# RMSNorm factors as fp32r products of two halves, and earlier sums for the feed-forward norm, in a two-layer decoder

## The chip, the cores and the metric

The kernel runs on one core of a Trainium2 chip. The metric is the device time of one execution in microseconds (us). The median of three runs of the kernel before is 2770.46 us (2770.25 to 2772.49). One further execution was recorded by the profiler, and everything read from a trace below comes from that one.

The core's engines run side by side and each takes its own instructions in order: TensorE (PE) multiplies matrices, and its weight loads are shown apart as PEld; VectorE (DVE) and ScalarE (ACT) do elementwise work; GpSimd (POOL) does a few small operations here; SyncE's queue (SP) issues the transfers. An instruction that waits for another engine holds up everything behind it on its own engine.

## The reference

Two layers, 2048 features, 256 tokens. Each layer mixes tokens (an SSD mixer in layer 0, forgetting attention in layer 1), then has a SwiGLU feed-forward block of 5632 hidden features and a gate that adds a projected per-layer input. Six kinds of RMSNorm stand around them:

```python
def rmsnorm(x, w):
    return x * lax.rsqrt(jnp.mean(x * x, axis=-1, keepdims=True) + EPS) * w

for i in range(DEPTH):
    hn = rmsnorm(h, norm_mix_pre[i])
    mix = ssd_mixer(...) if i % 2 == 0 else fox_mixer(...)
    h = h + rmsnorm(mix, norm_mix_post[i])
    ff = swiglu(rmsnorm(h, norm_ffn_pre[i]), w_gate, w_up, w_down)
    h = h + rmsnorm(ff, norm_ffn_post[i])
    pe = rmsnorm(p[i] @ ple_w_proj[i], ple_norm[i])
    h = h + jax.nn.sigmoid(h @ ple_w_gate[i]) * pe
```

The SSD mixer also normalizes its 4096 inner features in 8 groups of 512, and multiplies by a weight behind that. All is float32.

## The kernel before

**Data.** Activations lie transposed: a chunk is a tile of 128 features by 256 tokens, 16 chunks (h0 to h15) make the residual. A matrix product is made to float32 precision from fp32r products of two halves: a weight tile raw is cast to fp32r on ACT (wh, L181), and the rest raw minus wh is formed on DVE (wl, L186); an activation x likewise has a high half and a low half side by side in 512 columns. The high weights then multiply both halves (128x512, L243) and the low weights the high half (128x256, L245). ACT and DVE take the two halves of the result out of PSUM: a copy (tb, L270) and an addition (L271).

**Units and stages.** A unit is a group of up to six output chunks that are accumulated in PSUM side by side. A stage is one weight tile of a unit, with its transfer, its cast wh, its wl and its products. Units follow each other without a break, so that the next unit's first stages run while the last unit's results are still taken out. Weight tiles have numbers in the order of their use (wl264, wh548).

**What is done beside the products.** Small tasks stand in a queue, `bg`, and a few are popped with each stage. `paced` puts a task's DVE operation behind the wl of a stage that is named by `low`, `lag` does the same for ACT's side, `turn` holds the next wl behind a task's last operation. So the order on DVE and ACT is laid down by hand: a task that is popped a stage earlier stands ahead of another wl.

**A norm.** Squares of the 16 chunks are made on ACT (L293) and added on DVE (L294) into one tile (ssb, ssp for the per-layer projection, gss for the mixer's groups). `rstd_small` sums that tile over its 128 partitions by products whose stationary operand is the tile's half and whose moving operand is one column of ones (L314, float32), scales the sums on DVE (ms, L317) and raises them to the power -0.5 on POOL (rs, L320). `rstd_wide` spreads the factors of 256 tokens over all partitions: DVE makes two diagonal matrices (dg, L326), and a float32 product with a tile of ones gives 128x256 (L330), which ACT copies out (rwide, rpe or grw, L333). The trace shows each call of either as four hardware products, since it splits a float32 product in two. There are 18 calls of each.

**The places that the change touches.**

- The update unit is the first unit of the feed-forward block. While its products run, DVE makes the new residual from the mixer's normalized output: per chunk a scaling (sg, L458), an addition (h, L462) and the low half of the next block's input (x, L473); ACT makes the high half (L467).
- Behind it `late_norm` computes the feed-forward norm beside the next unit, the up unit: four pops of four squares and sums, `f1` with the column sum (wl263 to wl265), and `f2` with the wide product and the copy; then half of the factor (rwide2, L517), and the gate's silu in pops (L551 to L558). The norm's factor is applied to the results, since it is a factor per token.
- The per-layer norm (`pe_small`, `pe_wide`) runs beside the gate's units at the end of each layer, where the next chunks of h are formed (pp, L652; h, L656) once its factor rpe is there.
- The mixer's eight group norms (`gate_tasks`), the norm behind the mixer and the one behind the feed-forward block (`post_norm`, with `rstd_small` and `rstd_wide`), and the first norm of each layer.

Of the kernel before, what the change touches and what calls it, by code (L numbers as in the profile page):

```python
# [56 lines left out]
def tile_trunk(ctx, tc, a, out):  # L57
# [24 lines left out]
    ident, tri3, nstril, bigm = cst[:, 0:128], cst[:, 128:512], cst[:, 512:640], cst[:, 640:768]  # L82
    ones = cp.tile([P, P], F32, name="ones")
# [227 lines left out]
    def rstd_small(acc, n):  # L311
        ps = misc()
        for j in range(2):
            PE.matmul(ps[:, j:j + 1], lhsT=acc[:, j * P:(j + 1) * P], rhs=ones[:, :1],  # L314
                      start=True, stop=True)
        ms = tmp("ms", (P, 2))
        dmark[0] = V.tensor_scalar(out=ms, in0=ps[:, :2], scalar1=1.0 / n, scalar2=EPS,  # L317
                                   op0=mult, op1=add)
# [4 lines left out]
    def rstd_wide(rs, o):  # L323
        dg = tmp("dg", bufs=1)
        for j in range(2):
            dmark[0] = V.tensor_scalar(out=dg[:, j * P:(j + 1) * P], in0=ident,  # L326
                                       scalar1=rs[:, j:j + 1], scalar2=None, op0=mult)
        ps = misc()
        for j in range(2):
            PE.matmul(ps[:, j * P:(j + 1) * P], lhsT=ones, rhs=dg[:, j * P:(j + 1) * P],  # L330
                      start=True, stop=True)
# [31 lines left out]
    A.activation(warm, mhalf, AF.Exp)  # L363

# [137 lines left out]
    def mk_r(half=True, small=None, pin=False):  # L502
        r = []

        def f1():
            r.append(rstd_small(ssb, D))
# [5 lines left out]
        def f2():  # L512
            rstd_wide(r[0], rwide)
            if pin:
                lag[1].append(mark[0])
            if half:
                V.tensor_scalar(out=rwide2, in0=rwide, scalar1=0.5, scalar2=None, op0=mult)  # L517
        return f1, f2
# [19 lines left out]
    def tail(i, mpx, m, pp, mk_next):  # L538
# [3 lines left out]
        with ExitStack() as st:  # L542
# [24 lines left out]
            def late_norm():  # L567
                f1, f2 = mk_r(pin=True)
                bg.extend(sums_of(ssb, h, range(NCH), (4, 4, 4, 4)))
                bg.extend((f1, noop, f2, noop))  # L570
# [65 lines left out]

        def pe_small():
            r_pe.append(rstd_small(ssp, D))
            turn.append(dmark[0])
# [108 lines left out]
    def prep0(c):  # L748
        if c + 3 < NCH:
            load_x(c + 3)  # L750
        if c == 8:
            nc.sync.dma_start(out=cst, in_=a["cst"])
        split(h[c], xs0[c], col("mix_pre0", c))
        sumsq(ssb, h[c], c == 0)

    with ExitStack() as ys:
        yp = pool(ys, "yp", side="right")
        y = [yp.tile([P, T], F32, name=f"y{c}") for c in range(32)]
        with ExitStack() as st:
# [166 lines left out]
            def gate_tasks(g, S):  # L926
# [392 lines left out]
```

## Time and profile before

| | |
|---|---|
| median of three runs | 2770.46 us |
| the profiled execution | 2772.22 us |
| its span on the core | 2770.4 us |
| PE busy | 2759.2 us (100% of the span) |
| DVE busy | 1914.8 us (69%) |
| ACT busy | 1483.5 us (54%) |
| POOL busy | 50.3 us (2%) |
| granted TensorE clock | 1.0 in every slice |

A row of the timeline gives the start, the duration and the count of equal instructions in a row, and in brackets how long the engine was idle before and which instruction ended that. The ends of products are modelled and overlap the next start by some tenths of a microsecond, so distances of starts tell more than durations: a 128x512 product and the next start 0.23 us apart, a 128x256 fp32r product and the next 0.117 us. The idle time in brackets is by the same reason somewhat shorter than the time that the queue of products loses. On DVE an operation's successor starts some 0.08 us before the duration of the first is over.

### The profile page before, as it was taken

To read this page: it belongs to the slowest core of one execution; us is meant where nothing else is said; L and a number is where in the kernel's file an instruction comes from. 1 tells how busy PE (TensorE), PEld (TensorE's weight loads), DVE (VectorE), ACT (ScalarE), POOL (GpSimd) and SP (SyncE) were. 2 spreads that over 40 slices of the span, in tenths; PEclk is the share of its full clock that TensorE was granted. 3 is DMA by queue.
4 is the path that set the end of the run, shared out by engine and by line. 5 is a ranking of instruction groups with operands and counts; after the bars stand their busy time and mean duration, and the time that the engine had idled before them with its cause. 6 is when DMAs were issued, how large, how long until landed. Compare 5 with 4: busy or idle time off the path is not lost.

```text
span 2770.4 us, 43140 instructions
## 1 busy us (share of the span) xinstructions
PE 2759.2 (100%) x16342; PEld 2451.2 (88%) x16342; DVE 1914.8 (69%) x3145; ACT 1483.5 (54%) x2455; POOL 50.3 (2%) x104
## 2 busy tenths in 40 slices
PE   9999999999999999999999999999999999999999
PEld 8888888889888888888898998889888888888898
DVE  8888878755876645666668756766876545666577
ACT  6586676554654444444546544555654444445454
POOL 0000000000000000000000000000000000000000
PEclk9999999999999999999999999999999999999999
DMA  7665655565566555656545676545656556656544
GB/s 252 191 197 185 190 189 176 158 211 181 158 214 192 190 190 187 190 181 194 193 163 200 184 211 193 179 156 165 201 187 194 190 191 185 193 171 200 202 162 165
DMA packets 262512, 520.10 MB, mean 188 GB/s; under 512 B 17392, under 2 KB 42128, under 8 KB 262304
## 3 DMA queue, kind: packets, MB, share of 16 engines
q1 hardware_dynamic: 258640, 504.96, 57.5%
q0 software_dynamic: 3520, 12.15, 1.4%
q8 instruction: 128, 2.10, 0.3%
q14 instruction: 80, 0.66, 0.1%
q10 hardware_dynamic: 144, 0.24, 0.0%
HBM read 515.10 MB, written 2.18 MB: 187 GB/s over the span
## 4 chain that ended last, share of the span: by engine, by line
PE 97%; DVE 2%; ACT 1%; issue 0%; DMA 0%; SPq 0%; DVEq 0%; ACTq 0%
PE acc L243 56%; PE acc L245 30%; PE acc L240 1%; PE acc L239 1%; PE acc L238 1%; PE acc L232 1%; PE acc L233 1%; PE acc L234 1%; DVE wl L186 1%; PE mi L914 1%; PE mi L916 0%; PE mi L330 0%; PE mi L881 0%; PE mi L1152 0%; PE mi L1188 0%
## 5 line engine op out<-in xcount | busy, mean ns | idle before, releaser
L243 PE MATMUL acc<-x,wh 128*128 128x512 f32 x5008 | 1708.4, 394 | 5.3 <-DVE g L271 2.3
L186 DVE TENSOR_TENSOR wl<-raw,wh 128x1024 fp32r<-128x1024 f32 (+4 forms) x1020 | 1173.0, 1155 | 743.7 <-ACT wh L181 742.9
L181 ACT CAST wh<-raw 128x1024 fp32r<-128x1024 f32 (+4 forms) x1020 | 1006.3, 993 | 968.4 <-PE acc L243 851.6
L245 PE MATMUL acc<-x,wl 128*128 128x256 f32 x5008 | 1329.4, 283 | 0.2
L243 PEld LDWEIGHTS acc<-x,wh 128*128 128x128 f32 x5008 | 926.3, 188 | 190.6 <-issue 3.8
L245 PEld LDWEIGHTS acc<-x,wl 128*128 128x128 f32 x5008 | 932.2, 189 | 26.4 <-issue 2.1
L243 PE MATMUL acc<-a,wh 128*128 128x512 f32 x1232 | 425.5, 391 | 0.0
L245 PE MATMUL acc<-a,wl 128*128 128x256 f32 x1232 | 342.3, 282 | 0.0
L243 PEld LDWEIGHTS acc<-a,wh 128*128 128x128 f32 x1232 | 230.0, 188 | 46.5
L245 PEld LDWEIGHTS acc<-a,wl 128*128 128x128 f32 x1232 | 233.2, 189 | 2.2
L243 PE MATMUL acc<-xb,wh 128*128 128x512 f32 x512 | 181.9, 397 | 0.0
L270 ACT COPY tb<-acc 128x256 f32<-128x256 f32 (+1 forms) x401 | 140.2, 369 | 45.2 <-PE acc L245 27.3
L245 PE MATMUL acc<-xb,wl 128*128 128x256 f32 x512 | 146.0, 285 | 0.0
L243 PEld LDWEIGHTS acc<-xb,wh 128*128 128x128 f32 x512 | 96.0, 188 | 19.1
L245 PEld LDWEIGHTS acc<-xb,wl 128*128 128x128 f32 x512 | 97.0, 189 | 0.7 <-issue 0.2
L243 PE MATMUL acc<-xq,wh 128*128 128x512 f32 x224 | 77.7, 391 | 0.0
L896 ACT ACTIVATE E<-ab,bias 128x128 f32<-128x128 f32 x192 | 59.7, 390 | 13.7 <-PE mi L916 12.7
L271 DVE TENSOR_TENSOR g<-acc,tb 128x256 f32<-128x256 f32 x172 | 66.1, 417 | 0.6
L825 DVE SCALAR_TENSOR_TENSOR g<-xr,vec,g 128x256 f32<-128x256 f32 x144 | 63.3, 479 | 1.5 <-ACT g L822 0.8
L245 PE MATMUL acc<-xq,wl 128*128 128x256 f32 x224 | 63.1, 282 | 0.0
L320 POOL TENSOR_TENSOR rs<-ms,mhalf 128x2 f32<-128x2 f32 x18 | 24.4, 1356 | 1926.8 <-DVE ms L317 1926.8
L294 DVE TENSOR_TENSOR ssb<-ssb,sq 128x256 f32<-128x256 f32 x120 | 50.6, 422 | 12.0 <-ACT sq L293 8.1
(219 smaller groups left out, 2198.1 us busy)
## 6 DMA issues: line engine op xcount, KB each, us to landing
raw<-down SPq DMA_DIRECT2D x176, 512.0 KB, 4.1
raw<-ssd_in SPq DMA_DIRECT2D x152, 512.0 KB, 4.5
raw<-gate SPq DMA_DIRECT2D x128, 512.0 KB, 4.4
raw<-up SPq DMA_DIRECT2D x128, 512.0 KB, 4.4
raw<-fox_in SPq DMA_DIRECT2D x64, 512.0 KB, 4.1
raw<-gate SPq DMA_DIRECT2D x64, 384.0 KB, 3.2
raw<-up SPq DMA_DIRECT2D x64, 384.0 KB, 3.5
raw<-ssd_out SPq DMA_DIRECT2D x40, 512.0 KB, 4.3
```

Of the source, the lines that this page charges most:

```text
L181: low_a[0] = A.copy(out=wh[:, :kc * n], in_=raw[:, :kc * n])
L186: low[0] = V.tensor_tensor(out=wl[:, :kc * n], in0=raw[:, :kc * n], in1=wh.bitcast(F32)[:, :kc * n], op=sub)
L232: PE.matmul(o, lhsT=xh, rhs=wh[:, c, :], start=st, stop=False)
L233: PE.matmul(o, lhsT=xh, rhs=wl[:, c, :], start=False, stop=False)
L234: PE.matmul(o, lhsT=x[:, 1, t * P:(t + 1) * P], rhs=wh[:, c, :], start=False, stop=sp)
L243: PE.matmul(accs[t], lhsT=wh[:, c, t * P:(t + 1) * P], rhs=x.rearrange("p a n -> p (a n)"), start=st, stop=False)
L245: PE.matmul(accs[t][:, :T], lhsT=wl[:, c, t * P:(t + 1) * P], rhs=x[:, 0, :], start=False, stop=sp)
L270: i = A.copy(out=tb[:np_], in_=acc[:np_, T:2 * T])
L271: took[0] = (i, V.tensor_tensor(out=o, in0=acc[:np_, :T], in1=tb[:np_], op=add))
L294: last_v[0] = V.tensor_tensor(out=acc, in0=acc, in1=sq, op=add)
L825: V.scalar_tensor_tensor(out=c, in0=xr[:, k:k + T], scalar=col(f"conv_w{k}", cc), in1=c, op0=mult, op1=add)
L896: A.activation(E[:, i, b * P:(b + 1) * P], ab[:, i, lo:lo + P], AF.Relu, scale=-1.0, bias=bias3[:, b, h0 + i:h0 + i + 1])
```

## The change

The change has three parts.

- The wide product (`rstd_wide`): the factors are split on DVE into fp32r halves (rh and rl, 128x2 each). Instead of two diagonal matrices against ones, each half's column is taken as a stationary operand by broadcasting, against an fp32r identity (identr): four fp32r products. All 18 calls are changed.
- The column sum (`rstd_small`): 12 of the 18 calls get the tile split first, by a cast on ACT (`hi`) and a subtraction on DVE (`lo`), and each half's columns are summed by an fp32r product with two columns of ones: again four products. These are the 8 groups of the mixer, the 2 feed-forward norms and the 2 per-layer norms. The other 6 stay as they were.
- The order: of the feed-forward norm's 16 squares, 9 are popped during the update unit (after 13 empty pops) instead of behind it; behind it stand 4 and 3, then `f0` (hi), `f1` (lo and the column sum), `f2a` (the wide product alone), an empty pop and `f3` (the copy and rwide2, placed by hand). In the per-layer norm two more sums move ahead into the unit before, hi is its own pop, and the rest follows.

The diff, cut (line numbers of the kernel after are higher by 2 at L186, by 20 or so behind `rstd_wide`):

```diff
+    def halves(acc):
+        s = [tmp("sq", dt=F32R, bufs=4), tmp("sq", dt=F32R, bufs=4)]
+        def hi(pin=False):
+            with after(low_a[0]) if pin else nullcontext():
+                mark[0] = A.copy(out=s[0], in_=acc)
+            if pin:
+                lag[1].append(mark[0])
+        def lo():
+            last_v[0] = V.tensor_tensor(out=s[1], in0=acc, in1=s[0].bitcast(F32), op=sub)
+        return s, hi, lo
...
+    def rstd_small(acc, n, s=None):
...
+                for i in range(2):
+                    PE.matmul(ps[:, 2 * j:2 * j + 2], lhsT=s[i][:, js], rhs=onesr, start=i == 0,
+                              stop=i == 1)
...
     def rstd_wide(rs, o):
-        dg = tmp("dg", bufs=1)
-        for j in range(2):
-            dmark[0] = V.tensor_scalar(out=dg[:, j * P:(j + 1) * P], in0=ident,
-                                       scalar1=rs[:, j:j + 1], scalar2=None, op0=mult)
+        rr = [tmp("rh", (P, 2), F32R), tmp("rl", (P, 2), F32R)]
+        V.tensor_copy(out=rr[0], in_=rs)
+        dmark[0] = V.tensor_tensor(out=rr[1], in0=rs, in1=rr[0].bitcast(F32), op=sub)
         ps = misc()
         for j in range(2):
-            PE.matmul(ps[:, j * P:(j + 1) * P], lhsT=ones, rhs=dg[:, j * P:(j + 1) * P],
-                      start=True, stop=True)
+            for i in range(2):
+                PE.matmul(ps[:, j * P:(j + 1) * P],
+                          lhsT=rr[i][:, j:j + 1].broadcast_to((P, P)), rhs=identr,
+                          start=i == 0, stop=i == 1)
...
             def late_norm():
-                f1, f2 = mk_r(pin=True)
-                bg.extend(sums_of(ssb, h, range(NCH), (4, 4, 4, 4)))
-                bg.extend((f1, noop, f2, noop))
+                chain = mk_r(pin=True)
+                bg.extend(sums_of(ssb, h, range(9, NCH), (4, 3)))
+                bg.extend(chain)
...
+                    if first[0]:
+                        assert not bg
+                        bg.extend([noop] * 13 + sums_of(ssb, h, range(9), (3, 3, 3)))
...
-        pops0 = [noop] * 14 + [ssp_of(8, 9), ssp_of(10, 11)]
-        pops1 = [seq(ssp_of(12, 13), t1(0, 1)), seq(ssp_of(14, 15), t1(2, 3)),
+        pops0 = [noop] * 13 + [ssp_of(8, 9), ssp_of(10, 11), ssp_of(12, 13)]
+        pops1 = [seq(ssp_of(14, 15), t1(0, 1)), seq(pe_hi, t1(2, 3)),
                  seq(pe_small, t1(4, 5), t2(0, 1)), t2(2, 3), seq(pe_wide, t2(4, 5))]
```

How the instructions stand is shown at three places; each also occurs in layer 1. A row is the line, the operation, what it writes and what it reads; the numbers behind a tile's name tell instances apart.

**DVE, the feed-forward norm in layer 0** (mi is the column sum's result in PSUM). Before:

```order
L186 TENSOR_TENSOR wl264_8328<-raw264_8325,wh264_8327 128x768
L317 TENSOR_SCALAR ms_812_8346<-mi_811_8343 128x2
L186 TENSOR_TENSOR wl265_8353<-raw265_8350,wh265_8352 128x768
L186 TENSOR_TENSOR wl266_8371<-raw266_8368,wh266_8370 128x768
L186 TENSOR_TENSOR wl267_8397<-raw267_8394,wh267_8396 128x768
L326 TENSOR_SCALAR dg_814_8386<-cst_80,rs_813_8348 128x128 x2
L517 TENSOR_SCALAR rwide2_139<-rwide_138 128x256
L186 TENSOR_TENSOR wl268_8415<-raw268_8412,wh268_8414 128x768
L551 TENSOR_TENSOR sg_778_8177<-sg_778_8177,rwide2_139 128x256
```

After:

```order
L188 TENSOR_TENSOR wl263_8395<-raw263_8392,wh263_8394 128x768
L323 TENSOR_TENSOR sq_825_8309<-ssb_143,sq_824_8308 128x256
L337 TENSOR_SCALAR ms_840_8416<-mi_839_8411 128x2
L188 TENSOR_TENSOR wl264_8423<-raw264_8420,wh264_8422 128x768
L188 TENSOR_TENSOR wl265_8450<-raw265_8447,wh265_8449 128x768
L188 TENSOR_TENSOR wl266_8468<-raw266_8465,wh266_8467 128x768
L345 CAST rh_842_8438<-rs_841_8418 128x2
L346 TENSOR_TENSOR rl_843_8439<-rs_841_8418,rh_842_8438 128x2
L552 TENSOR_SCALAR rwide2_142<-rwide_141 128x256
L188 TENSOR_TENSOR wl267_8488<-raw267_8485,wh267_8487 128x768
```

The scaling ms stood behind wl264, and stands ahead of it now; rwide2, which reads the copied factor, stood behind wl267 and stands ahead of it now. On PE the column sum's last products stand as before right ahead of the first use of wl264, and the wide product stands ahead of the last of wl266's six low products, where it stood behind the first of wl267's.

**DVE, the end of the update unit in layer 0**, whose x_745 (before: x_720) is the last low half. Before:

```order
L473 SCALAR_TENSOR_TENSOR x_719_7686<-h14_97,vec_79,x_719_7686 128x256
L458 SCALAR_TENSOR_TENSOR sg_777_8106<-m0_15_6601,vec_79,rwide_138 128x256
L462 TENSOR_TENSOR h15_98<-h15_98,sg_777_8106 128x256
L186 TENSOR_TENSOR wl257_8125<-raw257_8122,wh257_8124 128x768
L473 SCALAR_TENSOR_TENSOR x_720_7687<-h15_98,vec_79,x_720_7687 128x256
L186 TENSOR_TENSOR wl258_8144<-raw258_8141,wh258_8143 128x768
L186 TENSOR_TENSOR wl259_8150<-raw259_8147,wh259_8149 128x768
L271 TENSOR_TENSOR sg_778_8177<-acc_756_7794,tb_779_8178 128x256
L271 TENSOR_TENSOR sg_780_8181<-acc_757_7795,tb_781_8182 128x256
```

After:

```order
L495 SCALAR_TENSOR_TENSOR x_744_7765<-h14_99,vec_79,x_744_7765 128x256
L480 SCALAR_TENSOR_TENSOR sg_803_8188<-m0_15_6680,vec_79,rwide_141 128x256
L484 TENSOR_TENSOR h15_100<-h15_100,sg_803_8188 128x256
L188 TENSOR_TENSOR wl257_8207<-raw257_8204,wh257_8206 128x768
L296 TENSOR_TENSOR ssb_143<-ssb_143,sq_804_8224 128x256
L495 SCALAR_TENSOR_TENSOR x_745_7766<-h15_100,vec_79,x_745_7766 128x256
L296 TENSOR_TENSOR ssb_143<-ssb_143,sq_805_8227 128x256
L188 TENSOR_TENSOR wl258_8233<-raw258_8230,wh258_8232 128x768
L188 TENSOR_TENSOR wl259_8239<-raw259_8236,wh259_8238 128x768
L296 TENSOR_TENSOR ssb_143<-ssb_143,sq_806_8266 128x256
L273 TENSOR_TENSOR sg_812_8284<-acc_782_7876,tb_813_8285 128x256
L273 TENSOR_TENSOR sg_814_8288<-acc_783_7877,tb_815_8289 128x256
```

Three sums into ssb now stand among the last low half, wl258, wl259 and the first addition that frees a PSUM tile, and more among the additions behind.

**DVE and PE, the per-layer norm in layer 0**, DVE first (gz are results of the gate, taken out of PSUM). Before:

```order
L648 SCALAR_TENSOR_TENSOR pp0_4_6606<-gz_1295_15493,pp0_4_6606 128x256
L648 SCALAR_TENSOR_TENSOR pp0_5_6607<-gz_1297_15497,pp0_5_6607 128x256
L326 TENSOR_SCALAR dg_1310_15644<-cst_80,rs_1309_15592 128x128 x2
L186 TENSOR_TENSOR wl547_15656<-raw547_15653,wh547_15655 128x1024
L652 SCALAR_TENSOR_TENSOR pp0_0_6602<-pp0_0_6602,vec_79,rpe_142 128x256
L656 TENSOR_TENSOR h0_83<-h0_83,pp0_0_6602 128x256
L186 TENSOR_TENSOR wl548_15681<-raw548_15678,wh548_15680 128x1024
```

After:

```order
L188 TENSOR_TENSOR wl547_15759<-raw547_15756,wh547_15758 128x1024
L345 CAST rh_1342_15744<-rs_1341_15692 128x2
L346 TENSOR_TENSOR rl_1343_15745<-rs_1341_15692,rh_1342_15744 128x2
L273 TENSOR_TENSOR gz_1345_15833<-acc_1331_15601,tb_1346_15834 128x256
L273 TENSOR_TENSOR gz_1347_15837<-acc_1332_15602,tb_1348_15838 128x256
L699 SCALAR_TENSOR_TENSOR pp0_0_6681<-pp0_0_6681,vec_79,rpe_145 128x256
L703 TENSOR_TENSOR h0_85<-h0_85,pp0_0_6681 128x256
L188 TENSOR_TENSOR wl548_15784<-raw548_15781,wh548_15783 128x1024
```

PE, where the wide product stands. Before:

```order
L245 MATMUL acc_1299_15501<-x_1229_14976,wl546_15625 128x256
L243 MATMUL acc_1300_15502<-x_1228_14975,wh546_15624 128x512
L330 MATMUL mi_1311_15647<-dg_1310_15644,ones_81 128x128 x2
L245 MATMUL acc_1300_15502<-x_1228_14975,wl546_15625 128x256
L243 MATMUL acc_1300_15502<-x_1229_14976,wh546_15624 128x512
L245 MATMUL acc_1300_15502<-x_1229_14976,wl546_15625 128x256
```

After:

```order
L247 MATMUL acc_1333_15603<-x_1259_15068,wl547_15759 128x256
L350 MATMUL mi_1344_15748<-identr_81,rl_1343_15745 128x128
L350 MATMUL mi_1344_15748<-identr_81,rh_1342_15744 128x128
L350 MATMUL mi_1344_15748<-identr_81,rl_1343_15745 128x128
L245 MATMUL acc_1333_15603<-x_1260_15069,wh547_15758 128x512
L247 MATMUL acc_1333_15603<-x_1260_15069,wl547_15759 128x256
L247 MATMUL acc_1334_15604<-x_1259_15068,wl547_15759 128x256
L245 MATMUL acc_1334_15604<-x_1260_15069,wh547_15758 128x512
L247 MATMUL acc_1334_15604<-x_1260_15069,wl547_15759 128x256
L245 MATMUL acc_1355_15851<-x_1245_15054,wh548_15783 128x512
L245 MATMUL acc_1356_15852<-x_1245_15054,wh548_15783 128x512
L247 MATMUL acc_1353_15849<-x_1245_15054,wl548_15784 128x256
```

Between the wide product and the first use of wl548 stood 29 products, and 7 stand there now. On DVE wl548 stands behind the first product with rpe (pp) and the addition into h0, as before; in layer 1 it is behind two of each and one more addition out of PSUM.

## Rows read from the trace of the kernel before

**Rows 1.** The page: its span, busy time by engine, chain that ended last.

```profile
span 2770.4 us, 43140 instructions
...
PE 2759.2 (100%) x16342; PEld 2451.2 (88%) x16342; DVE 1914.8 (69%) x3145; ACT 1483.5 (54%) x2455; POOL 50.3 (2%) x104
...
PE 97%; DVE 2%; ACT 1%; issue 0%; DMA 0%; SPq 0%; DVEq 0%; ACTq 0%
```

**Rows 2.** Waits of PE: us in total, times, longest.

```profile
PE acc L243 <- DVE g L271: 2.3, 2, 1.2
PE acc L243 <- ACT wh L181: 1.8, 3, 0.6
```

**Rows 3.** Groups by line and shape: busy us, mean ns, idle before.

```profile
L243 PEld LDWEIGHTS acc<-x,wh 128*128 128x128 f32 x5008 | 926.3, 188 | 190.6 <-issue 3.8 <-DVE g L271 2.7 <-ACT wh L181 2.5
...
L330 PEld LDWEIGHTS mi<-dg,ones 128*128 128x128 f32 x72 | 10.3, 190 | 0.6
```

**Rows 4.** Timeline (start, duration, count) of PE: wide product, per-layer norm, layer 0.

```profile
1498.98 0.61 PE L330 MATMUL mi<-dg,ones 128*128 128x128 f32 x4
...
1499.54 0.40 PE L243 MATMUL acc<-x,wh 128*128 128x512 f32 x1
```

**Rows 5.** Timeline of PE, a float32 product of 256 columns (L1152).

```profile
1680.63 0.60 PE L1152 MATMUL mi<-k,q 128*128 128x256 f32 x2
...
1681.18 0.39 PE L243 MATMUL acc<-xb,wh 128*128 128x512 f32 x1
```

**Rows 6.** Timeline of DVE and PE, behind the feed-forward norm's column sum in layer 0.

```profile
750.46 0.16 DVE L317 TENSOR_SCALAR ms<-mi 128x2 f32<-128x2 f32 x1
750.50 0.73 PE L245 MATMUL acc<-x,wl 128*128 128x256 f32 x4
750.54 0.96 DVE L186 TENSOR_TENSOR wl<-raw,wh 128x768 fp32r<-128x768 f32 x1
```

**Rows 7.** Timeline of PE, ACT and DVE, that norm's wide product and copy.

```profile
757.01 0.61 PE L330 MATMUL mi<-dg,ones 128*128 128x128 f32 x4
...
757.65 0.37 ACT L333 COPY rwide<-mi 128x256 f32<-128x256 f32 x1 [6.93 <-PE mi L330]
...
758.06 0.29 DVE L517 TENSOR_SCALAR rwide<-rwide 128x256 f32<-128x256 f32 x1 [4.43 <-ACT rwide L333]
758.81 0.95 PE L243 MATMUL acc<-x,wh 128*128 128x512 f32 x3 [0.60 <-ACT wh L181]
```

**Rows 8.** Timeline of PE, the end of the up unit.

```profile
770.82 0.86 PE L245 MATMUL acc<-x,wl 128*128 128x256 f32 x6
772.84 0.50 PE L243 MATMUL acc<-x,wh 128*128 128x512 f32 x1 [1.16 <-DVE g L271]
```

**Rows 9.** By stretch: length, busy PE, PEld, DVE, ACT, POOL, clock, DMA share, GB/s.

```profile
758.06:772.36 14.30, 13.02 (x74) 11.07 (x72) 13.76 (x26) 9.96 (x17) 0.00 (x0) 1.00 0.69 223
716.00:735.00 19.00, 19.00 (x108) 16.29 (x107) 18.65 (x35) 11.79 (x21) 0.00 (x0) 1.00 0.67 181
```

**Rows 10.** Timeline of DVE, the end of the update unit in layer 0.

```profile
732.97 0.48 DVE L473 SCALAR_TENSOR_TENSOR x<-h,vec,x 128x256 fp32r<-128x256 f32 x1
...
735.24 0.75 DVE L271 TENSOR_TENSOR sg<-acc,tb 128x256 f32<-128x256 f32 x2
```

**Rows 11.** Timeline of DVE, first results of the gate's first unit, layer 0.

```profile
1479.90 0.42 DVE L294 TENSOR_TENSOR ssp<-ssp,sq 128x256 f32<-128x256 f32 x1
1480.24 0.75 DVE L271 TENSOR_TENSOR gz<-acc,tb 128x256 f32<-128x256 f32 x2
```

**Rows 12.** Timeline of DVE behind the per-layer norm's copy, layer 0.

```profile
1500.03 0.48 DVE L652 SCALAR_TENSOR_TENSOR pp<-pp,vec,rpe 128x256 f32<-128x256 f32 x1 [3.22 <-ACT rpe L333]
...
1500.89 1.22 DVE L186 TENSOR_TENSOR wl<-raw,wh 128x1024 fp32r<-128x1024 f32 x1
```

**Rows 13.** Timeline of PE and DVE, the per-layer norm's wide product, layer 1.

```profile
2727.15 0.61 PE L330 MATMUL mi<-dg,ones 128*128 128x128 f32 x4
...
2728.99 0.76 DVE L656 TENSOR_TENSOR h<-h,pp 128x256 f32<-128x256 f32 x2
```

More of the change, by code (lines that the diff above doesn't have):

```diff
@@ L309, in paced @@
         return r
-    def rstd_small(acc, n):
+    def halves(acc):
[9 more added lines that the diff above has]
+    def rstd_small(acc, n, s=None):
         ps = misc()
         for j in range(2):
-            PE.matmul(ps[:, j:j + 1], lhsT=acc[:, j * P:(j + 1) * P], rhs=ones[:, :1],
-                      start=True, stop=True)
+            js = slice(j * P, (j + 1) * P)
+            if s is None:
+                PE.matmul(ps[:, j:j + 1], lhsT=acc[:, js], rhs=ones[:, :1], start=True, stop=True)
+            else:
+                for i in range(2):
+                    PE.matmul(ps[:, 2 * j:2 * j + 2], lhsT=s[i][:, js], rhs=onesr, start=i == 0,
+                              stop=i == 1)
         ms = tmp("ms", (P, 2))
-        dmark[0] = V.tensor_scalar(out=ms, in0=ps[:, :2], scalar1=1.0 / n, scalar2=EPS,
-                                   op0=mult, op1=add)
+        dmark[0] = V.tensor_scalar(out=ms, in0=ps[:, :2] if s is None else ps[:, :4:2],
+                                   scalar1=1.0 / n, scalar2=EPS, op0=mult, op1=add)
         rs = tmp("rs", (P, 2), bufs=3)
@@ L363, in tile_trunk @@
     A.activation(warm, mhalf, AF.Exp)
+    A.copy(out=onesr, in_=ones[:, :2])
     def load_x(c):
@@ L503, in mk_r, with f0 @@
         r = []
+        s, hi, lo = halves(ssb) if pin else (None, None, None)
+        def f0():
+            hi(True)
         def f1():
-            r.append(rstd_small(ssb, D))
+            if pin:
+                paced(lo)
+            r.append(rstd_small(ssb, D, s))
             if pin:
@@ L513, in f2, with f2a, f3, halved @@
             rstd_wide(r[0], rwide)
-            if pin:
-                lag[1].append(mark[0])
             if half:
                 V.tensor_scalar(out=rwide2, in0=rwide, scalar1=0.5, scalar2=None, op0=mult)
-        return f1, f2
+        def f2a():
+            r.append(rstd_wide(r[0], None))
+        def f3():
+            with after(low_a[0]):
+                lag[1].append(A.copy(out=rwide, in_=r[1]))
+            def halved():
+                last_v[0] = V.tensor_scalar(out=rwide2, in0=rwide, scalar1=0.5, scalar2=None,
+                                            op0=mult)
+            paced(halved)
+        return (f0, f1, f2a, noop, f3) if pin else (f1, f2)
     def out_units(sizes, rhs, m_of, pre=None):
@@ L635, in ssp_of, with pe_hi @@
             return f
+        hs = []
+        def pe_hi():
+            hs.extend(halves(ssp))
+            hs[1](True)
         def pe_small():
-            r_pe.append(rstd_small(ssp, D))
+            paced(hs[2])
+            r_pe.append(rstd_small(ssp, D, hs[0]))
             turn.append(dmark[0])
@@ L752, in prep0 @@
             nc.sync.dma_start(out=cst, in_=a["cst"])
+        if c == 12:
+            A.copy(out=identr, in_=ident)
         split(h[c], xs0[c], col("mix_pre0", c))
@@ L926, in gate_tasks, with gn0 @@
             def gate_tasks(g, S):
+                def gn0():
+                    S["s"], hi, S["lo"] = halves(S["ss"])
+                    hi()
                 def gn1():
-                    S["rs"] = rstd_small(S["ss"], 512)
+                    S["lo"]()
+                    S["rs"] = rstd_small(S["ss"], 512, S["s"])
                 def gn2():
```

7 lines of the change are left out of this document (4 added, 3 removed).

## Prediction

> **What bounds the kernel now.** I read the page first. PE is busy for the whole span and the chain that ended last is 97% PE [rows 1], so the time is what PE's queue takes, plus its gaps. An edit elsewhere counts only where it makes PE wait or spares it a wait. The waits of PE come next: the two largest are the addition that frees a PSUM tile (2.3 us in 2 places) and the cast wh (1.8 us in 3) [rows 2]. Both belong to the feed-forward norm, so I looked there on the timeline of each engine. Lastly I asked where DVE has no room. In the up unit's silu pops it works 13.76 of 14.30 us, in the update unit 18.65 of 19.00 [rows 9], and the change puts or moves DVE work into both.
>
> **The products themselves.** A wide product is four pieces before and after. From the first piece to the next-but-one product it takes 0.56 us [rows 4]; one 128x256 product lies between (0.117 us), which leaves 0.443, or 0.111 a piece. The fp32r main product's weight load takes 188 ns and the float32 piece's 190 [rows 3], so I take the new pieces at 0.111 as well: both are 128x128 loads with a short product behind. The column sum has four pieces before and after too. This term is 0. Its bounds: an fp32r product of 256 columns costs 0.117, so if only columns counted a piece would cost 0.056 to 0.06; if a piece went as a float32 product of 256 columns does, two of which take 1681.18 - 1680.63 - 0.117 = 0.43 us [rows 5], it would cost 0.217. These ends are rivals below.
>
> The 12 splits add a cast on ACT and a subtraction on DVE of about 0.4 us each, like other 128x256 operations there. In the mixer's groups both engines have idle time and their result is due a stage later, so I cost them at 0; without that cover each would be 0.4 us.
>
> **Feed-forward norm: the column sum.** ms waits for PE's last summing piece, and wl264 now stands behind it on DVE. Before, wl264 was ready and PE took it at 750.50; the wl behind ms started at 750.54 and ran 0.96 [rows 6]. In its place wl264 is ready at 750.50 + 0.05 for the signal: 751.55. PE's low products are due at 750.50, and nothing else stands in PE's queue, so they are 1.05 us later: **+2.1** in the two layers. No order on PE hides it, since the pieces stand right ahead of these products.
>
> **Feed-forward norm: the copy.** Before, the copy waited for the wide product and the cast wh268 stood behind it. The wide product starts at 757.01, four pieces and five products of 0.117 end at 758.04, and PE goes on at 758.81 [rows 7]: 0.77 us lost, twice. After, the wide product stands before one low product, six high products of wl267's stage and its six low ones: 0.44 + 0.12 + 1.37 + 0.70 = 2.6 us until wh268 is needed. The copy ends 1.0 us after the first piece, the cast takes 0.8, so this stall goes: **-1.5**. What is late next is wl267, which now stands behind rwide2. rwide2 starts 1.05 us behind the first piece [rows 7], its successor 0.21 later, and that wl takes 0.96 + 0.05: 2.27. PE needs it after 0.44 + 0.12 + 1.37 = 1.93. That is 0.34 each: **+0.7**.
>
> **End of the up unit.** PE's six low products from 770.82 end at 771.52 and it goes on at 772.84 [rows 8], 1.32 us lost to a DVE that is full from the factor's arrival on. The factor comes some 1.6 us of PE work earlier (six high products and two low ones), but wl267, 0.87 us of DVE, is moved behind it. At most 0.75 each comes back and at least 0; silu's other steps wait on ACT as well, so I take 0.3: **-0.6**.
>
> **Update unit.** DVE is full there [rows 9] and gets three additions among the last low half, two wl and the first addition that frees PSUM. An addition costs 0.34 from start to start [rows 11]. One stands ahead of the last low half, which was done at 733.45 just as PE took it [rows 10], and two more ahead of the first PSUM addition at 735.24 [rows 10]. Three would be 1.0 us if PE had no slack; I take 0.85: **+1.7**, ends 0 and 2.0. The additions leave the next unit, where no stall hung on them.
>
> **Per-layer norm.** Two more additions into ssp stand ahead of the first gz addition, and PE waits on that one already. There is one pop more between: 0.34 each, **+0.7**.
>
> Then the wide product itself. It stood far ahead of the first use of wl548 and now has, behind the first piece, the other pieces with a low product between (0.56), two high and three low products (0.81) and two high ones (0.46) until wl548 is needed: 1.83 us. On DVE the chain is known from before: first piece 1498.98 [rows 4], pp at 1500.03, wl started at 1500.89 and ran 1.22 [rows 12], which is 3.13 us. With the low product between and the signal it is 3.30: 1.47 us of stall. In layer 1 two pp stand ahead; the first addition into h started 1.84 us after the first piece [rows 13], and with that addition, a PSUM addition and a second one (0.34 each) and wl's 1.22 it is 4.08 + 0.17 = 4.25: 2.42 us of stall. Together **+3.9**. I find nothing that hides it: wl548 cannot pass pp on DVE, and PE has no other product ready.
>
> **Small places.** In the per-layer norm ms stands ahead of wl545 with its products a little nearer (+0.35 by the order, end 1), a mixer group's last scaling of four y moves ahead of a low half (+0.4, ends 0 and 1.9), and the dg pair on four post norms' path becomes two 128x2 operations (-0.3): **+0.45**. Two new copies at the head, of ones and of the identity, stand on ACT where PE is the later engine: 0, at most 0.4.
>
> **Sum.** 2.1 - 1.5 + 0.7 - 0.6 + 1.7 + 0.7 + 3.9 + 0.45 = +7.45 us on the profiled execution's 2772.22, 2779.7. The median of the runs shown lies 1.8 us lower, so the forecast is **2778 us**, +0.27%.
>
> **Rivals.**
> - *Fp32r loads are faster.* The pieces then cost 0.056 to 0.06 instead of 0.111. 18 wide products and 12 sums of four pieces are 120 pieces: -6.4 us, 2771.5. The load times speak against it: 188 ns for fp32r, 190 for float32 [rows 3]. The Trainium skill, page "TensorE: Matmul & The Clock Gate", section "Weight-path perf modes — Fast Weight Load (FWL) and DoubleRow", says that fast weight load is on for 128 weights whose type is not FP32; by that rule fp32r could count as such and this rival would hold, though the same table says that four-byte weights win nothing. The trace's two load times do not show a difference between the types.
> - *Fp32r products of 128 columns take longer than their load.* At 0.217 a piece, 72 wide pieces add 7.6 us: 2785.5. For it: the trace has no fp32r product under 256 columns, so its rate is not shown. Against it: at 256 and 512 columns the cost is proportional to the columns.
> - *The other side: DVE's new waits are covered.* The price is that of wl264, wl267 and wl548 behind their waits, 2.1 + 0.7 + 3.9 = 6.7 us. If PE had two weight tiles' halves ready ahead at these points, each wait under some 1.4 us would vanish, all but a third of this goes, and the time is 2771.5 less 1 to 3: 2768 to 2771, not slower. It decides at the distance of the wide product from wl548: 3.3 us of PE work there instead of 1.83 would do. The order of PE speaks against it.
> - *The copy is not moved far enough.* It stays ahead of wh268 on ACT, behind two squares. If the 0.77 stayed, 2779.5, slower still.
>
> **How the numbers follow.** A measurement of this kernel can tell some 0.2% from no change, which is 5.5 us: faster is below 2764.9, slower above 2776.0. Forecast, with an uncertainty of some 3 us from its terms: 0.70, of which 0.15 lies under 2776. Faster loads 0.10 (no change). Slow narrow products 0.12 (slower). Covered waits 0.08, of which half together with faster loads, which is faster (2771.5 - 6.4 and below). The last rival is within the forecast. That gives slower 0.67, no change 0.29, faster 0.04. The range goes from 2769 (forecast of the first rival with its spread) to 2786 (the second).
>
> **What would show it.** In the changed kernel's waits of PE: a wait of about 1.0 us for wl ahead of L247 behind the feed-forward column sum; none of 0.6 for a cast behind the copy; waits of about 1.4 and 2.3 us for wl at the end of the gate unit with the wide product; L273's wait a little under 1.2. Four pieces of L350 should stand 0.11 apart. The prediction is wrong if these pieces stand nearer 0.06 or 0.2 apart, if the gate unit's wide product is followed by no wait, or if DVE's additions in the update unit run without a gap on PE.

## The result and the profile after

| | before | after |
|---|---|---|
| median, us | 2770.53 (2770.24 to 2772.49, 7 runs) | 2779.85 (2778.22 to 2781.92, 7 runs) |
| profiled execution, us | 2772.22 | 2781.73 |
| its span, us | 2770.4 | 2780.0 |

The ratio is 1.0033, 95% interval 1.0023 to 1.0042: slower by 9.3 us. The forecast was 2778 us with a range of 2769 to 2786. Executions of one kernel lie in groups some 1.5 to 2 us apart (of after 2778.2 to 2778.3, 2779.8 and 2781 to 2782), so medians under 2 us apart are read here together with the lowest runs, which for these two kernels differ by 2778.22 - 2770.24 = 8.0 us.

The page of after, to be read beside [rows 1]:

```profile
span 2780.0 us, 43161 instructions
...
PE 2763.2 (99%) x16342; PEld 2445.7 (88%) x16342; DVE 1913.3 (69%) x3157; ACT 1485.2 (53%) x2469; POOL 47.4 (2%) x104
...
PE 94%; DVE 5%; issue 1%; ACT 0%; DMA 0%; SPq 0%; DVEq 0%
```

PE issues the same number of products in both kernels. Its busy time grows by 4.0 us though the span grows by 9.6, so more than half of the loss is idle time of PE, and DVE's share of the chain rises from 2% to 5%. The waits of PE in after (engine, tile, what it waited for: us in total, times, longest) say for what:

```profile
PE acc L247 <- DVE wl L188: 5.7, 4, 2.2
PE acc L245 <- DVE g L273: 1.8, 2, 0.9
...
PE acc L245 <- DVE gz L273: 1.0, 2, 0.5
PE acc L245 <- DVE sg L273: 0.8, 2, 0.4
```

Against [rows 2] the wait for the cast wh is gone, that for g has fallen from 2.3 to 1.8, and a wait for wl that was not in the list before is now the largest: twice behind a feed-forward norm's column sum, twice behind a per-layer norm's wide product. The rows left out stand at the kernel's head. PE and DVE of after around the first of them, in order of time (start, duration, count, idle time before and what ended it), answer to [rows 6]:

```profile
744.40 1.48 DVE L296 TENSOR_TENSOR ssb<-ssb,sq 128x256 f32<-128x256 f32 x3
...
747.32 0.17 PE L334 MATMUL mi<-onesr,sq 128*128 128x2 f32 x1
747.53 0.42 DVE L323 TENSOR_TENSOR sq<-ssb,sq 128x256 fp32r<-128x256 f32 x1
...
751.64 0.39 PE L334 MATMUL mi<-onesr,sq 128*128 128x2 f32 x3
752.06 0.16 DVE L337 TENSOR_SCALAR ms<-mi 128x2 f32<-128x2 f32 x1 [4.11 <-PE mi L334]
752.14 2.70 DVE L188 TENSOR_TENSOR wl<-raw,wh 128x768 fp32r<-128x768 f32 x3
753.15 0.38 PE L247 MATMUL acc<-x,wl 128*128 128x256 f32 x1 [1.13 <-DVE wl L188]
```

DVE stands idle for 4.11 us on ms with wl264 right behind it, while PE works through 24 products; then PE comes to wl264's products and finds nothing ready. The column sum itself stands in two places: the one piece that needs the cast alone for the first 128 tokens at 747.32, the other three 4.32 us later.

The four pieces of the wide product stand 0.11 us apart, and the copy behind them no longer stops PE, where [rows 7] showed 0.77 us lost:

```profile
758.21 0.27 PE L350 MATMUL mi<-identr,rh 128*128 128x128 f32 x1
758.32 0.28 PE L350 MATMUL mi<-identr,rl 128*128 128x128 f32 x1
758.43 0.34 PE L247 MATMUL acc<-x,wl 128*128 128x256 f32 x1
758.60 1.56 PE L245 MATMUL acc<-x,wh 128*128 128x512 f32 x6
760.25 0.97 PE L247 MATMUL acc<-x,wl 128*128 128x256 f32 x6
```

Six high products from 758.60 take 1.40 us, so 0.25 us is lost ahead of 760.25. At the end of the up unit PE waits 0.81 us where it waited 1.16 [rows 8], and in the update unit 0.39 us where it did not wait:

```profile
774.60 0.51 PE L245 MATMUL acc<-x,wh 128*128 128x512 f32 x1 [0.81 <-DVE g L273]
```

```profile
737.42 0.50 PE L245 MATMUL acc<-x,wh 128*128 128x512 f32 x1 [0.39 <-DVE sg L273]
```

The per-layer norm in layer 0 and, below it, in layer 1 (PE):

```profile
1506.63 0.63 PE L245 MATMUL acc<-x,wh 128*128 128x512 f32 x2
1508.49 0.38 PE L247 MATMUL acc<-x,wl 128*128 128x256 f32 x1 [1.23 <-DVE wl L188]
```

```profile
2738.23 0.63 PE L245 MATMUL acc<-x,wh 128*128 128x512 f32 x2
2741.03 0.47 PE L247 MATMUL acc<-x,wl 128*128 128x256 f32 x1 [2.16 <-DVE wl L188]
2741.30 0.63 PE L245 MATMUL acc<-x,wh 128*128 128x512 f32 x1
2741.73 0.63 PE L247 MATMUL acc<-x,wl 128*128 128x256 f32 x2
```

Two high products take 0.46 us, so 1508.49 - 1506.63 - 0.46 = 1.40 us is lost in layer 0 and 2741.03 - 2738.23 - 0.46 = 2.34 us in layer 1. Behind the second wait a high product takes 0.43 us where it took 0.23. The windows of that stretch and of one just ahead (length, busy PE, PEld, DVE, ACT, POOL, granted clock, DMA share, GB/s):

```profile
2736.00:2738.40 2.40, 2.40 (x18) 2.21 (x17) 1.29 (x4) 1.70 (x7) 0.00 (x0) 1.00 0.38 145
2740.78:2744.30 3.52, 3.27 (x12) 2.89 (x13) 3.52 (x9) 0.42 (x1) 0.00 (x0) 0.56 0.62 212
```

The products run at the lower of the two levels (1.2 GHz) until about 2744.5. Twelve products in that window instead of some 20 cost about 1.5 us.

### The profile page after: what moved, and what is told of

Its sections match the earlier page's. It is cut to its first block, busy times and chain, and to the rows that moved or that the text cites. A ratio compares the mean times of both kernels' runs of the same rounds, so it can differ in the third digit from the quotient of the medians.

```text
span 2780.0 us, 43161 instructions
## 1 busy us (share of the span) xinstructions
PE 2763.2 (99%) x16342; PEld 2445.7 (88%) x16342; DVE 1913.3 (69%) x3157; ACT 1485.2 (53%) x2469; POOL 47.4 (2%) x104
## 4 chain that ended last, share of the span: by engine, by line
PE 94%; DVE 5%; issue 1%; ACT 0%; DMA 0%; SPq 0%; DVEq 0%
PE acc L245 54%; PE acc L247 28%; DVE wl L188 3%; PE acc L241 1%; PE acc L242 1%; PE acc L240 1%; PE acc L234 1%; PE acc L236 1%; PE acc L235 1%; PE mi L963 1%; DVE sg L480 0%; DVE x L495 0%; PE mi L965 0%; DVE pn L480 0%; PE mi L930 0%
## 5 line engine op out<-in xcount | busy, mean ns | idle before, releaser
L590 ACT ACTIVATE th<-sg 128x256 f32<-128x256 f32 x88 | 33.3, 421 | 44.3 <-DVE sg L588 44.2
```

The source lines that it names most:

```text
L590: mark[0] = A.activation(th, sg, AF.Tanh)
```

## The experiments

The theory was that the order decides: products cost the same, and the loss is DVE's queue at the places above. The rivals were that the new precision itself costs (narrow fp32r products, splits), and that one of the moved steps alone is to blame. The first group of runs takes the change apart, the second moves one place at a time.

**One part at a time.** Before's order with the fp32r wide product and the splits of the mixer's 8 groups; the other column sums stay float32:

```diff
-    def rstd_small(acc, n):
+    def halves(acc):
...
+    def rstd_small(acc, n, s=None):
...
-                return [noop, gn1, gn2] if g < NG - 1 else [gn1, noop, gn2, noop]
+                return [gn0, gn1, gn2] if g < NG - 1 else [gn0, gn1, noop, gn2, noop]
```

> The kernel before in its own order, with the 18 wide products and the 8 column sums of the mixer's groups as fp32r products of two halves; the sums of the feed-forward and per-layer norms stay float32, and no pop is moved. Theory 'order' (the change costs time by the places of its DVE work, its products cost what the old ones did): 2770.5 to 2771.5, at most 0.5 of the 9.3 us; pieces 0.11 us apart, no wait of PE for wl over 0.3 us. Rival 'precision' (halves are slower by themselves, on PE or by the splits): 2774 or more.

Measured: 2771.42 (2770.96 to 2772.93, 11 runs) against 2770.57, ratio 1.0003 (0.9994 to 1.0012). The 104 fp32r pieces (72 of the wide products, 32 of the mixer's sums) and the mixer's splits move the median by 0.85 us and the lowest run by 0.9. By the interval they cost 3.3 us at most, and PE's list has no wait for wl. So the narrow products are not what makes most of the loss.

The order alone: all of after's pops, the later copy and the early sums, with float32 products and no split.

```diff
-        return f1, f2
+        return (f0, f1, f2a, noop, f3) if pin else (f1, f2)
...
+                        bg.extend([noop] * 13 + sums_of(ssb, h, range(9), (3, 3, 3)))
...
+        pops0 = [noop] * 13 + [ssp_of(8, 9), ssp_of(10, 11), ssp_of(12, 13)]
```

> The changed kernel's pops with the products of the kernel before: sums begun in the update unit, sums of the per-layer norm moved ahead, copy later, but all wide products and column sums float32, with no splits between. By the order of its instructions the column sum then stands a stage earlier on PE than in the changed kernel, the wide products early, and all silu steps ahead of the up unit's end. Theory 'chain' (the pops pay, and what costs is that the splits add steps to the norm's chain, so that each later step slips behind a wl): before's waits of 0.77 and 1.32 a layer go, the update unit's 0.9 a layer and 0.6 ahead of gz come: 2770.5 - 4.2 + 2.4 = 2768.7. Theory 'pops' (the moved pops cost by themselves): 2776 or more.

Measured: 2768.90 (2768.59 to 2770.59, 11 runs) against 2770.80, ratio 0.9993 (0.9984 to 1.0002). Lowest against lowest it is 1.7 us under before. The moved pops and the later copy lose nothing by themselves. Its waits of PE:

```profile
PE acc L243 <- DVE gz L271: 1.0, 2, 0.5
PE acc L243 <- DVE sg L271: 0.8, 2, 0.4
PE acc L243 <- DVE g L271: 0.7, 2, 0.3
```

The costs of the early sums (sg, gz) are there in the same size as in after. What is missing is the wait for wl, and g has fallen to 0.7. The column sum and ms of this kernel:

```profile
741.80 1.48 DVE L294 TENSOR_TENSOR ssb<-ssb,sq 128x256 f32<-128x256 f32 x3
...
744.75 0.50 PE L314 MATMUL mi<-ones,ssb 128*128 128x1 f32 x4
...
745.28 0.16 DVE L317 TENSOR_SCALAR ms<-mi 128x2 f32<-128x2 f32 x1 [0.27 <-PE mi L314]
```

All four pieces stand 2.95 us behind the start of the last additions, and DVE waits 0.27 us for them. In after those additions start at 744.40: the first piece stands 2.92 us behind them, the other three 7.24.

That points at the split sums, so two kernels undo one kind of product each in after. First only the column sums of the feed-forward and per-layer norms, 4 in all, go back to float32 (wide products and the mixer's 8 sums stay split, the order stays):

```diff
-            hi(True)
+            pass
-            if pin:
-                paced(lo)
-            r.append(rstd_small(ssb, D, s))
+            r.append(rstd_small(ssb, D))
...
-            paced(hs[2])
-            r_pe.append(rstd_small(ssp, D, hs[0]))
+            r_pe.append(rstd_small(ssp, D))
```

> The changed kernel with one thing undone: the column sums of the feed-forward and per-layer norms (4 of 18) are float32 again, without cast and subtraction; the wide products stay fp32r halves, the mixer's sums split, the pops as changed. Theory 'split sums' (the cast and the subtraction ahead of a column sum put its norm's chain behind one more wl, and that alone turns the moved pops from a gain into a loss): e9's 2768.9 plus the 0.8 of e1: 2769.3 to 2770. Rival 'split factors' (rh and rl ahead of the wide product do it): 2774 or more.

Measured: 2769.74 (2769.32 to 2771.23, 11 runs) against 2770.79, ratio 0.9995 (0.9987 to 1.0004). These four splits are worth 2779.85 - 2769.74 = 10.1 us by the medians and 2778.22 - 2769.32 = 8.9 by the lowest runs. Its waits for gz, sg and g are those of the order-only kernel to the tenth, and none is for wl. DVE and PE at its sum:

```profile
742.54 1.47 DVE L296 TENSOR_TENSOR ssb<-ssb,sq 128x256 f32<-128x256 f32 x3
...
745.46 0.50 PE L331 MATMUL mi<-ones,ssb 128*128 128x1 f32 x4
```

Again 2.92 us. The edit takes out the cast, the subtraction and the places that the kernel gives them in the queues, all at once.

Then the reverse: the wide products go back to a float32 diagonal (dg), all 12 sums stay split.

```diff
-        rr = [tmp("rh", (P, 2), F32R), tmp("rl", (P, 2), F32R)]
...
+        dg = tmp("dg", bufs=1)
...
+            PE.matmul(ps[:, j * P:(j + 1) * P], lhsT=ones, rhs=dg[:, j * P:(j + 1) * P],
+                      start=True, stop=True)
```

> The changed kernel with the other thing undone: all 18 wide products are float32 with diagonal matrices again, the column sums stay split, the pops as changed. Theory 'split sums': the same waits as in the changed kernel, 1.3 us ahead of wl264's products, 1.5 and 2.4 or more ahead of wl548's and wl1008's, 2778 to 2781. Rival 'split factors': 2772 or less.

Measured: 2779.38 (2777.93 to 2779.63, 7 runs), ratio 1.0030 (1.0018 to 1.0041), as slow as after. Its largest wait of PE is the one for wl, longer than in after:

```profile
PE acc L246 <- DVE wl L187: 6.8, 6, 2.4
```

The later copy alone, in before:

```diff
-                bg.extend((f1, noop, f2, noop))
+                bg.extend(chain)
```

where `chain` is `(f1, f2a, noop, f3)`.

> The kernel before with one part of the change alone: the feed-forward norm's factor is copied later, behind the cast wh268, all products float32 as before, sums where they were. Theory 'order': the wait of 0.77 us for wh268 goes in both layers; DVE's queue, which is full until the up unit's end, starts only 0.44 earlier, so 0.3 of each comes back there: 2770.5 less 0.9, 2769.6. Rival 'the copy is worth its whole wait': 2769.0; rival 'all is given back at the up unit's end': 2770.5.

Measured: 2769.99 (2769.18 to 2771.47, 11 runs), ratio 0.9995 (0.9986 to 1.0003); lowest against lowest 1.0 us under before. The two waits for wh behind the copy are gone (a third, in layer 0's mixer, is left), and part of them comes back one step later, at the end of the up unit:

```profile
PE acc L243 <- DVE g L271: 3.1, 2, 1.5
```

Last, the better order from these readings: the order-only kernel with the per-layer pops as before and 8 early sums instead of 9, one pop later.

```diff
-                bg.extend(sums_of(ssb, h, range(9, NCH), (4, 3)))
+                bg.extend(sums_of(ssb, h, range(8, NCH), (4, 4)))
-                        bg.extend([noop] * 13 + sums_of(ssb, h, range(9), (3, 3, 3)))
+                        bg.extend([noop] * 14 + sums_of(ssb, h, range(8), (4, 4)))
-        pops0 = [noop] * 13 + [ssp_of(8, 9), ssp_of(10, 11), ssp_of(12, 13)]
+        pops0 = [noop] * 14 + [ssp_of(8, 9), ssp_of(10, 11)]
```

> As e9, with the per-layer norm's pops as in the kernel before and only 8 of the 16 sums begun in the update unit, one stage later (two pops of four), so that none stands ahead of its last low half and one ahead of the first addition out of PSUM. Theory 'chain': the 0.6 ahead of gz goes and the update unit's waits fall from 0.9 to some 0.3 to 0.5 a layer: 2767 to 2767.5, below both kernels. If the update unit's cost hangs on the number of sums and not on their place: 2768.

Measured: 2767.01 (2766.65 to 2768.90, 11 runs) against 2770.80, ratio 0.9985 (0.9976 to 0.9994): faster than both kernels, and 3.7 us under before by the lowest runs. The waits at sg and gz fall from 0.8 and 1.0 to 0.4 and 0.2:

```profile
PE acc L243 <- DVE sg L271: 0.4, 2, 0.2
PE acc L243 <- DVE gz L271: 0.2, 1, 0.2
```

**One place at a time, in after.** The per-layer norms' wide product one pop earlier:

```diff
+            turn.append(dmark[0])
...
-                 seq(pe_small, t1(4, 5), t2(0, 1)), t2(2, 3), seq(pe_wide, t2(4, 5))]
+                 seq(pe_small, t1(4, 5), t2(0, 1)), seq(pe_wide, t2(2, 3)), t2(4, 5)]
```

> The changed kernel with one thing altered: the per-layer norm's wide product is popped one stage earlier and the next wl is held behind its halves on DVE, so that 29 products stand between it and the first use of wl548, as in the kernel before. Theory 'order': the waits of 1.4 and 2.3 us and the slow stretch behind the second go, 9.3 less 3.7 to 5.5: 2774.3 to 2776. Rival 'the per-layer norm is late for another reason' (column sum, additions): no wait goes, 2778 or more.

Measured: 2774.11 (2773.75 to 2776.20, 11 runs), 5.7 us under after, ratio to before 1.0014 (1.0006 to 1.0023). Only the two waits behind the feed-forward sums are left:

```profile
PE acc L247 <- DVE wl L188: 2.3, 2, 1.1
```

The stalls taken away were 1.40 + 2.34 = 3.7 us; the lowest runs differ by 4.5, the medians by 5.7. The rest, 0.8 to 2 us, was not taken apart. The stretch at the lower clock behind the longer wait, some 1.5 us in the executions that have it, can be part of it in the medians.

ms one pop later, so that it stands behind wl264:

```diff
-            if pin:
-                paced(lo)
...
+        def fl():
+            paced(lo)
...
-        return (f0, f1, f2a, noop, f3) if pin else (f1, f2)
+        return (f0, fl, f1, f2a, f3) if pin else (f1, f2)
```

> The changed kernel with the feed-forward norm's low half and its column sum popped one after the other, so that ms stands behind wl264 on DVE as before the change; the wide product moves a few products later, the copy stays. Theory 'order': the wait of 1.3 us ahead of wl264's products falls to 0.2, 2 x 1.1 = 2.2 us in two layers, of which up to 0.6 is lost again to a later factor: 9.3 less 1.6 to 2.2, 2777.7 to 2778.3. Rival 'DVE is full there anyway' (what wl264 gains is lost at the next wl or at the up unit's end): 2779.5 or more.

Measured: 2778.96 (2777.49 to 2780.49, 8 runs), 0.9 us under after, 0.7 by the lowest runs. That is between the two expectations. The wait behind the column sum is gone, but the edit also took the empty pop behind the wide product, and rwide2 now holds wl267 up:

```profile
756.74 0.29 DVE L553 TENSOR_SCALAR rwide<-rwide 128x256 f32<-128x256 f32 x1 [4.31 <-ACT rwide L550]
756.95 0.95 DVE L188 TENSOR_TENSOR wl<-raw,wh 128x768 fp32r<-128x768 f32 x1
```

```profile
757.96 0.97 PE L247 MATMUL acc<-x,wl 128*128 128x256 f32 x6 [0.92 <-DVE wl L188]
```

What is spared at one norm step is paid at the next: the chain has to be moved as a whole.

Both edits together:

> The changed kernel with both repairs, the per-layer norm's wide product early and ms behind wl264. If the terms add up: 2774.1 (wide product early alone) less 1.6 to 2.2: 2772 to 2772.5, still above the kernel before by the update unit's 1.8, the additions ahead of gz and the mixer's places, less the copy's and the up unit's gain. If they don't: 2773.5 or more.

Measured: 2774.76 (2773.05 to 2775.12, 11 runs), ratio 1.0011 (1.0002 to 1.0020). The expected further gain did not come: against the wide product alone the median is 0.65 higher and the lowest run 0.7 lower, which tells nothing apart.

One pp instead of two ahead of wl in layer 1, and two instead of one in layer 0, to see the size of the per-layer wait follow DVE's queue:

```diff
-            pops1 += [t3(0, 1), t3(2, 3), t3(4, 5)]
+            pops1 += [t3(0), t3(1, 2), t3(3, 4, 5)]
```

> The changed kernel with layer 1's first rpe pop cut to one chunk, so that one pp and one addition into h stand ahead of wl1008 instead of two of each and an addition out of PSUM: the wait there should fall from 2.3 to about 1.4 us. Theory 'clock': behind the shorter wait the granted clock stays at its upper level, and the time falls by 0.9 plus up to 1.7 us: 2777.3, all runs close together. Rival 'wait alone' (the slow products behind the wait come from something else, such as transfers or PSUM): 0.9 us falls, products behind it still 0.43 and 0.21 us apart, 2779.

Measured: 2779.94 (2778.01 to 2780.17, 6 runs). The wait in layer 1 falls from 2.16 to 1.23, the value of layer 0, and no lower clock follows in this execution. But the steps pushed back hold up the next two wl, by 0.19 and 0.27, and the median stays. The forecast of a gain missed; no run is above 2780.2 where after has three above 2781.

```profile
2739.69 0.38 PE L247 MATMUL acc<-x,wl 128*128 128x256 f32 x1 [1.23 <-DVE wl L188]
```

```diff
-            pops1 += [t3(0), seq(t4(0), t3(1)), seq(t4(1), t3(2))]
+            pops1 += [t3(0, 1), t4(0), seq(t4(1), t3(2))]
```

> The changed kernel with layer 0's first rpe pop made as layer 1's: two pp, two additions into h and one out of PSUM ahead of wl548, so that the wait there should rise from 1.4 to about 2.3 us. Theory 'clock': behind this wait too the granted clock falls to its lower level for some 3.5 us, and the time rises by 0.9 plus up to 1.7 us: 2781 to 2783. Rival 'something of layer 1 alone': products behind the wait keep 0.23 and 0.117 us, 2780.8.

Measured: 2781.10 (2779.87 to 2782.60, 5 runs), 1.25 us over after (lowest 1.65). The wait in layer 0 is 2.17 us now, as in layer 1. In this execution neither was followed by a lower clock; the window behind layer 1's:

```profile
2740.20:2743.70 3.50, 2.98 (x17) 2.42 (x17) 3.50 (x8) 1.34 (x2) 0.00 (x0) 1.00 0.61 197
```

All 16 feed-forward sums behind the update unit again:

```diff
-                bg.extend(sums_of(ssb, h, range(9, NCH), (4, 3)))
+                bg.extend(sums_of(ssb, h, range(NCH), (4, 4, 4, 4)))
...
-                        bg.extend([noop] * 13 + sums_of(ssb, h, range(9), (3, 3, 3)))
```

> The changed kernel with the feed-forward norm's 16 sums all behind the update unit again (four pops of four), which puts the factor two pops later than in the changed kernel and one later than before. Theory 'trade': the update unit's waits (0.9 a layer) go, but silu's steps start later in a stretch where DVE is full, and the wait at the up unit's end rises from 1.0 to 2.2 to 2.9 us a layer: 2780.5 to 2782. Rival 'the early sums only cost': 1.8 us falls, 2778.

Measured: 2782.19 (2782.04 to 2783.75, 5 runs), ratio 1.0040 (1.0028 to 1.0053). The update unit's wait for sg is gone, but the whole chain is later, and the wait for g, 1.8 us in after, is 4.2 here; at the end of the up unit:

```profile
773.65 0.50 PE L245 MATMUL acc<-x,wh 128*128 128x512 f32 x1 [2.12 <-DVE g L273]
```

So the early sums, 1.8 us in the update unit, are worth more than they cost: without them the median is 2.3 us higher and the lowest run 3.8. Not all of that is waiting: in this execution the products behind the wait shown run at the lower clock (0.63 from 773.40 to 776.80).

## Why the prediction was right, point by point

Direction, size and places came out as forecast. "Measured" is how much later the same product runs in after's trace than in before's across the place, in both layers together; each is read to some 0.1 to 0.2 us, and they add to 9.9 where the two profiled executions differ by 9.5. Without the stretch at the lower clock these differ by some 8.0, and the forecast's sum was 7.45.

| step | forecast, us | measured, us |
|---|---|---|
| the products themselves | 0 | 0, pieces 0.11 apart |
| column sum, ms ahead of wl264 | +2.1 | +1.8 |
| copy, with wl267 behind rwide2 | -0.8 | -1.0 |
| end of the up unit | -0.6 | -0.6 |
| update unit | +1.7 | +1.8 |
| two more ssp additions ahead of gz | +0.7 | +0.6 |
| per-layer wide product | +3.9 | +4.3, and some 1.5 for the lower clock |
| small places | +0.45 | about +1.5 |

*The products.* That an fp32r piece costs what the float32 one cost, 0.11, was right, and both rivals on the products are out: the pieces are at 0.11, neither 0.06 nor 0.22, and the run with the parts of precision alone moved by 0.85 us, which its interval does not tell from nothing. The Trainium skill, page "TensorE: Matmul & The Clock Gate", section "Weight-path perf modes — Fast Weight Load (FWL) and DoubleRow", turns the fast load on for 128 weights that are not FP32. This trace shows no faster load for fp32r, whose groups in after stand at 188 and 190 ns:

```profile
L350 PEld LDWEIGHTS mi<-identr,rh 128*128 128x128 f32 x36 | 6.8, 188 | 0.3
L350 PEld LDWEIGHTS mi<-identr,rl 128*128 128x128 f32 x36 | 6.8, 190 | 0.2
```

*The waits.* All four waits for wl stand where the prediction put them: "about 1.0 us" behind the column sums is 1.13, "about 1.4 and 2.3" behind the wide products is 1.40 and 2.34 lost. The wait for the cast is gone. The two rivals with covered waits and an unmoved copy are out.

*Slips in the working.* In the column sum's term, wl264 is ready at 751.50 + 0.05, not 750.50 + 0.05; the result of 751.55 is right. The rival with covered waits gives 2768 to 2771, but two thirds of its 6.7 us taken from 2778 leave 2773.5; the waits that were measured rule it out at either price.

*Mis-sized.* The copy's place kept 0.25 us where 0.34 was expected. The small places are three times their term: in the distances between the two traces the start of the FoX part (about +0.5), a mixer group's scaling (+0.5) and the head (+0.3) are the larger ones, against -0.35 where two waits of before ended, with smaller ones beside them; no run took them apart. And the per-layer term counted the wait alone. In the profiled execution the stretch at 1.2 GHz behind the 2.16 us wait comes on top, which no row of before could price and which not every execution has.

*What the prediction had not seen.* It put each term to the place where the wait appears, and it priced the splits at nothing beyond their own instructions. The order-only run shows that the same pops without split sums are 1.9 us faster than before, and the kernel with the four sums in float32 keeps that gain but for 0.84. So the four splits, as the kernel places them, are the cause upstream. The subtraction lo stands behind two wl on DVE (747.53), and on PE the three pieces that need it, or come behind one that does, stand 24 products behind the first. Part of that is order and not waiting: lo is done at 747.95, the pieces come at 751.64. They stand 7.24 - 2.95 = 4.3 us later behind the last additions than in the order-only kernel, and ms, the factor, the wide product and the copy come behind them. No run kept the splits and moved lo or the pieces forward, so how much of the 4.3 us is the split and how much its place stays open.

From before to after the medians go: order -1.9; wide products and the mixer's splits 2769.74 - 2768.90 = +0.84, and +0.85 in before's order, so hardly another value in either order; the four splits of the feed-forward and per-layer sums +10.1 (8.9 by the lowest runs). Whether these four splits would cost as much in before's order was not run, nor were the two norms' splits run apart.

## What to carry to other kernels

Where the engine of products is full, an edit to a small side chain is priced by what stands behind its steps in the other engines' queues: look for the step that waits for PE and carries PE's next operand right behind it. Splitting an operand in two adds a cast and a subtraction ahead of the product; the product then waits for the slower half, and at a chain with no slack this costs several times its instructions: here 9 to 10 us for four splits of 0.41 us on ACT and 0.42 on DVE. Where the result is due a stage later it costs little: the mixer's eight splits and the 18 wide products came to 0.85 us together. Move a chain as a whole, and undo the parts of a mixed change one by one: here a gain of 1.9 us was hidden under a loss about five times its size.

## What the runs showed of the hardware that was not expected

One idle stretch of PE of 2.16 us was followed by 3.5 us at a granted clock of 0.56, with 512-column products 0.43 apart instead of 0.23. Past the kernel's head, five of the 14 profiled executions have idle stretches of PE of more than 2 us, eight in all. Behind five of these (2.12 to 2.37 us) such products stand 0.43 apart, behind three (2.09, 2.17 and 2.17 us) they keep 0.23. Behind none of the shorter ones, up to 1.63 us, does the distance change. What decides between the eight stays open.

At the start of the kernel, too, five of the 14 executions run some 3 to 4 us of their first products at the lower level (1.2 GHz), and nine run all of them at the upper (2.4 GHz). PE in the profiled executions of before and of the order-only kernel:

```profile
7.17 0.63 PE L243 MATMUL acc<-x,wh 128*128 128x512 f32 x1
7.60 0.41 PE L245 MATMUL acc<-x,wl 128*128 128x256 f32 x1
7.81 0.63 PE L243 MATMUL acc<-x,wh 128*128 128x512 f32 x1
```

```profile
7.13 0.40 PE L243 MATMUL acc<-x,wh 128*128 128x512 f32 x1
7.36 0.28 PE L245 MATMUL acc<-x,wl 128*128 128x256 f32 x1
7.48 0.40 PE L243 MATMUL acc<-x,wh 128*128 128x512 f32 x1
```

A pair takes 0.64 us in the one and 0.35 in the other. The granted clock of the record can miss this: for the stretch from 7.5 to 10.5 it reads 1.00 in before, and 0.50 in the run with the parts of precision alone, where as many products (11) run.

```profile
7.50:10.50 3.00, 3.00 (x11) 2.52 (x11) 3.00 (x8) 3.00 (x9) 0.00 (x0) 1.00 0.99 351
```

```profile
7.50:10.50 3.00, 3.00 (x11) 2.52 (x11) 3.00 (x8) 3.00 (x9) 0.00 (x0) 0.50 0.99 314
```

So distances of starts tell the clock more surely than the record does. Read by them, the six profiled executions without any stretch at the lower level lie within 0.9 us of their kernel's fastest run, and the eight with one or two such stretches 1.4 to 3.5 us above it.
